# A 31-tap convolution on TensorE: two tiles with four taps stacked on the rows, in place of one tile with diagonals

## The chip, the cores and the metric

The kernel runs on one core of a Trainium2 chip. The metric is the device time of one execution in microseconds; of a kernel the median of several runs is given. The core has five engines that work side by side, each through its own queue in order: TensorE (PE: matmuls; PEld is its weight loads), VectorE (DVE), ScalarE (ACT), GpSimd (POOL) and SyncE (SP), which here issues all transfers between DRAM and the on-chip memory. Matmul results land in PSUM, which has eight banks of 128 rows by 512 float32 values; everything else on chip lies in SBUF, 128 rows wide.

## The reference

One inference step of a two-layer decoder for a prompt of 512 tokens and eight sample sequences of eight tokens, 576 columns in all. Layer 0 mixes with a Conformer convolution and sliding-window attention, layer 1 with a Mamba-2 scan; each layer ends in a gated feed-forward block. What matters here is the Conformer branch of layer 0, cut to its core:

```python
a_val, a_gate, q, k, v = jnp.split(h @ w_in, [...], axis=-1)
u = a_val * jax.nn.sigmoid(a_gate)
padded = jnp.concatenate([conv_hist, u], axis=1)          # 30 earlier rows, then u
c = jax.nn.silu(layernorm(causal_dwconv(padded, conv_w, conv_b), ln_g, ln_b))
...
out = jnp.concatenate([c, o], axis=-1) @ w_out            # o: the attention's output
```

The convolution is depthwise: each of 512 channels has its own 31 taps, and its output at a position is the sum of 31 products over that position and the 30 before it. For the prompt the 30 earlier rows are zeros, for each sample sequence they come from a state.

## The kernel before

Activations lie transposed: channels on the 128 rows, the 576 token columns along the free dimension (512 of the prompt, then 8 x 8 of the samples). The 512 channels of the convolution are four tiles, numbered 0 to 3. Most large matmuls split both float32 factors into a high and a low part and add three products (`mm3`, lines 158 to 160); a plain float32 matmul appears in the trace as two records. Weights come in through `wr` (three buffers), are split by ScalarE (line 148) and VectorE (149) and then used.

`mix0` is the first mixer. `units` projects gate, value, query, key and value tiles from the normalized input. For convolution tile i, `a_gate(i)` makes the sigmoid and `a_val(i)` writes the product u into `cap[i]` (30 columns of zeros, then 512 prompt columns, 542 in all) and into `cas_v[i]` (eight sequences of 30 + 8 columns, 304 in all). Tiles 0 and 2 come first, then q, k and v, then tiles 1 and 3; the value projections of these two run inside the loop over the attention.

Then there are two ways to convolve.

Tiles 0, 2 and 3 run on VectorE. `segment(i)` lets ScalarE copy the tile into 72 overlapping windows of 38 columns (lines 397 and 398), so that prompt and samples have one form, and a later loop makes 31 multiply-adds of 128 x 576 for each tile (lines 681 and 683).

Tile 1 (`PC = 1`) runs on TensorE in `pe_conv`. `cap[1]` is split into a high and a low part, `cph`. For each of the 31 taps ScalarE makes two 128 x 128 diagonals of the tap's weights, high and low (line 522), and TensorE adds three matmuls of 512 columns into one PSUM bank (524 to 526). For the samples ScalarE makes a third diagonal in plain float32 (528), used in a matmul of 64 columns into a second bank (529). VectorE later brings both into `ca[1]` with the bias (673 and 674).

The loop over `todo` goes through eight attention units (four query blocks of 128, two key heads). `scores` multiplies queries and keys (581) into the ring "sc" of three PSUM banks and starts the softmax on VectorE and ScalarE (555 to 566); `values` transposes the probabilities (598), copies them out (600) and multiplies them with the values (602). Values of a unit are written after the scores of the next one. The taps of tile 1 are spread over the last six units. After the loop come the keys and values of the samples' caches (629, 630, loads by SP), their scores (640, 642) and value products (653, 655). At the end the LayerNorm over the four `ca` tiles starts with means by TensorE (691), and `out_proj` multiplies first the attention's output `oh`, then the convolution's output `cc`.

The order in which this is written is not the order in the queues. Before anything runs, a planner goes through the instructions by priority, which is the order of writing, and by the times at which it expects inputs to be ready, and fixes for each engine, SP included, one order. On the chip each engine follows its order and waits at the head of its queue. Buffers named by `self.S` are slots taken from a list in turn, `NSLOT` of them in this phase; a tile written into a slot waits until the slot's earlier readers are done.

Of the kernel before, what the change touches and what calls it, by code (L numbers as in the profile page):

```python
# [25 lines left out]
for _name, _w in (  # L26
    ("norm_e", 8), ("norm_o", 8), ("norm_f0", 8), ("norm_f1", 8),
    ("ca_w", 4 * 31), ("ca_b", 4), ("ln_g", 4), ("ln_b", 4), ("q_g", 1), ("k_g", 1),
    ("fw0", NF * 3), ("fb0", NF), ("fw1", NF * 3), ("fb1", NF),
    ("cc_w", 24 * 4), ("cc_b", 24), ("dsk", 16), ("gn", 16),  # L30
    ("sink_p", 8), ("sink_s", 2), ("dtb", 32), ("alog", 32),
):
    PV[_name] = _n
    _n += _w
# [4 lines left out]
for _name, _w in (  # L39
    ("ident", 128), ("prot", 128), ("blk2", 2), ("amask", 256), ("smask", 2 * 192),  # L40
    ("tri", 128), ("tris", 64), ("bmat", 64), ("bsel", 8), ("selx", 256), ("selm", 128),
    ("sel3", 192), ("bsel3", 4),
):
    CV[_name] = _n
    _n += _w
# [3 lines left out]
class Builder:  # L49
    NSLOT = 50  # L50
    EXTRA = 8
# [298 lines left out]
    def mix0(self):  # L350
# [49 lines left out]
        def a_val(i):  # L400
            def go(half, p):
# [3 lines left out]
                else:  # L405
# [104 lines left out]
        pconv = {}  # L510

        def pe_conv(k0, k1):

            i = PC
            if not pconv:
                pconv[0] = self.pm(), self.pm()
            pp, ps = pconv[0]
            for k in range(k0, k1):
                dg = []
                for w in (cwh, cwl):  # L520
                    dg.append(self.segp.tile([P, P], F32R, tag="dg", bufs=4, name="dg"))
                    nc.scalar.activation(dg[-1], self.ident, AF.Copy, scale=w.bitcast(F32)[:, k:k + 1])
                sl = slice(k, k + NP)
                nc.tensor.matmul(pp, dg[0], cph[0][:, sl], start=k == 0, stop=False)  # L524
                nc.tensor.matmul(pp, dg[0], cph[1][:, sl], start=False, stop=False)
                nc.tensor.matmul(pp, dg[1], cph[0][:, sl], start=False, stop=k == 30)
                df = self.segp.tile([P, P], F32, tag="df", bufs=2, name="df")
                nc.scalar.activation(df, self.ident, AF.Copy, scale=self.pv("ca_w", i * 31 + k))
                nc.tensor.matmul(bt(ps[:, 0:64]), df, cas_v[i][:, :, k:k + 8], start=k == 0, stop=k == 30)
# [94 lines left out]
        values(n, kv, pr)  # L624

# [44 lines left out]
        for i in range(4):  # L670
            if i == PC:
                pp, ps = pconv[0]
                nc.vector.tensor_scalar(ca[i][:, :NP], pp, self.pv("ca_b", i), None, op0=ADD)
                nc.vector.tensor_scalar(ca[i][:, NP:], ps[:, 0:64], self.pv("ca_b", i), None, op0=ADD)
                continue
# [26 lines left out]
        self.free(oh, list(ca.values()), list(cap.values()), cas, lrs, csq, *cph)  # L702
# [406 lines left out]
def build(nc, tc, d):  # L1109
    from contextlib import ExitStack  # L1110
    with ExitStack() as stack:
        b = Builder(nc, tc, d, stack)
        b.setup()
        with tc.tile_pool(name="segp", bufs=1) as b.segp:
            b.phase(b.segp, "prot", "tri")
# [11 lines left out]
def constants():  # L1127
# [12 lines left out]
    put("prot", prot)  # L1140
    half = np.arange(P) // 64
# [125 lines left out]
```

## Time and profile before

| | |
|---|---|
| median of 3 runs | 1622.1 us (1620.45 to 1622.54) |
| the profiled execution | 1617.26 us |
| its span, first to last instruction | 1615.5 us |
| TensorE busy | 1588.7 us (98%) |
| VectorE busy | 1026.3 us (64%) |
| ScalarE busy | 696.5 us (43%) |
| GpSimd busy | 109.4 us (7%) |
| granted TensorE clock, mean | 0.996 |

The profile is of one execution. L158 means line 158 of the kernel before. In a row of groups, `out<-in` names what an instruction writes and reads, xN is the number of instructions, and behind the bar stand busy microseconds in total, the mean of one in nanoseconds, and how long the engine stood idle just before them, with what ended the idling. In a timeline row stand start, duration, engine, line and operation; a bracket at the end gives idle time before it. Matmuls overlap in a pipeline, so the distance between two starts tells more than a duration. Rows of busy time in a stage give the stage, its length, and for PE, PEld, DVE, ACT and POOL the busy time and number of instructions, then the granted clock, the busy share of the DMA engines and GB/s. A row of SPq is SP issuing a transfer; rows of transfers give their number, size, and the median time from issue to landing.

### The profile page before, as it was taken

To read this page: it belongs to the slowest core of one execution; us is meant where nothing else is said; L and a number is where in the kernel's file an instruction comes from. 1 tells how busy PE (TensorE), PEld (TensorE's weight loads), DVE (VectorE), ACT (ScalarE), POOL (GpSimd) and SP (SyncE) were. 2 spreads that over 40 slices of the span, in tenths; PEclk is the share of its full clock that TensorE was granted. 3 is DMA by queue.
4 is the path that set the end of the run, shared out by engine and by line. 5 is a ranking of instruction groups with operands and counts; after the bars stand their busy time and mean duration, and the time that the engine had idled before them with its cause. 6 is when DMAs were issued, how large, how long until landed. Compare 5 with 4: busy or idle time off the path is not lost.

```text
span 1615.5 us, 28735 instructions
## 1 busy us (share of the span) xinstructions
PE 1588.7 (98%) x11704; PEld 1504.8 (93%) x11704; DVE 1026.3 (64%) x1847; ACT 696.5 (43%) x1333; POOL 109.4 (7%) x322
## 2 busy tenths in 40 slices
PE   8999999999999999999999999999899999999999
PEld 8996699999999999998997998998799999999999
DVE  7898677654365355578796676676776653554552
ACT  7248654322122122378766556557352221221220
POOL 0000001000000000010301101101110000000000
PEclk9999999999999999999999999999899999999999
DMA  7222022222222222224335325234222222222222
GB/s 229 71 73 69 1 66 90 80 91 79 80 90 70 93 87 76 83 72 141 132 82 166 102 70 176 92 97 156 97 69 89 91 80 79 92 71 87 92 80 76
DMA packets 63633, 150.05 MB, mean 93 GB/s; under 512 B 18558, under 2 KB 19582, under 8 KB 63502
## 3 DMA queue, kind: packets, MB, share of 16 engines
q1 hardware_dynamic: 63502, 148.23, 28.8%
q8 instruction: 92, 1.51, 0.4%
q14 instruction: 39, 0.32, 0.1%
HBM read 133.86 MB, written 14.34 MB: 92 GB/s over the span
## 4 chain that ended last, share of the span: by engine, by line
PE 89%; DVE 5%; ACT 4%; DMA 2%; issue 1%; POOL 0%; SPq 0%; DVEq 0%; ACTq 0%
PE mm L158 25%; PE mm L160 25%; PE mm L159 25%; DVE cconv L734 1%; DMA acb<-acd 1%; PE yp L974 1%; ACT wh L148 1%; PE pst L923 1%; PE po L602 1%; PE sc L581 1%; PE pt L180 1%; PE pyo L987 1%; PE yp L972 1%; PE mm L524 1%; PE pr L191 1%
## 5 line engine op out<-in xcount | busy, mean ns | idle before, releaser
L158 PE MATMUL mm<-hh,wh 128*128 128x288 f32 (+1 forms) x2288 | 680.6, 298 | 8.4 <-ACT wh L148 7.7
L160 PE MATMUL mm<-hh,wl 128*128 128x288 f32 x2288 | 679.8, 297 | 0.1
L159 PE MATMUL mm<-hl,wh 128*128 128x288 f32 (+1 forms) x2288 | 677.9, 297 | 0.0
L148 ACT ACTIVATE wh<-wr 128x1024 fp32r<-128x1024 f32 (+1 forms) x215 | 223.4, 1039 | 544.1 <-issue 283.3
L158 PEld LDWEIGHTS mm<-hh,wh 128*128 128x128 f32 (+1 forms) x2288 | 429.6, 188 | 14.8 <-ACT wh L148 8.0
L160 PEld LDWEIGHTS mm<-hh,wl 128*128 128x128 f32 x2288 | 429.7, 188 | 4.6 <-issue 2.8
L159 PEld LDWEIGHTS mm<-hl,wh 128*128 128x128 f32 (+1 forms) x2288 | 429.8, 188 | 3.5 <-issue 1.4
L149 DVE TENSOR_TENSOR wl<-wr,wh 128x1024 fp32r<-128x1024 f32 (+1 forms) x215 | 257.7, 1199 | 78.3 <-ACT wh L148 78.1
L158 PE MATMUL mm<-yh,wh 128*128 128x288 f32 x960 | 286.8, 300 | 2.5 <-ACT yh L168 2.5
L159 PE MATMUL mm<-yl,wh 128*128 128x288 f32 x960 | 287.6, 300 | 0.0
L160 PE MATMUL mm<-yh,wl 128*128 128x288 f32 x960 | 286.1, 299 | 0.0
L158 PEld LDWEIGHTS mm<-yh,wh 128*128 128x128 f32 x960 | 182.1, 190 | 6.9 <-issue 3.3
L159 PEld LDWEIGHTS mm<-yl,wh 128*128 128x128 f32 x960 | 182.1, 190 | 4.4 <-issue 3.2
L160 PEld LDWEIGHTS mm<-yh,wl 128*128 128x128 f32 x960 | 181.8, 190 | 2.9 <-issue 2.8
L257 DVE TENSOR_TENSOR x<-x,mm 128x288 f32<-128x288 f32 x192 | 85.7, 451 | 154.8 <-PE mm L160 154.4
L302 DVE TENSOR_TENSOR gbuf<-mm,rs 128x224 f32<-128x224 f32 x44 | 17.2, 392 | 108.0 <-PE mm L160 108.0
L313 ACT ACTIVATE gsilu<-gconv,par 128x512 f32<-128x512 f32 x44 | 31.8, 724 | 115.1 <-DVE gconv L310 115.1
L310 DVE SCALAR_TENSOR_TENSOR gconv<-gbuf,par,gconv 128x592 f32<-128x592 f32 x88 | 73.1, 831 | 1.5
L323 DVE TENSOR_TENSOR gsilu<-mm,gsilu 128x288 f32<-128x288 f32 x88 | 40.0, 455 | 50.3 <-PE mm L160 50.3
L683 DVE SCALAR_TENSOR_TENSOR ca<-seg,par,ca 128x576 f32<-128x576 f32 x90 | 71.3, 810 | 0.3
L734 DVE SCALAR_TENSOR_TENSOR cconv<-cbuf,par,cconv 128x600 f32<-128x600 f32 x72 | 61.4, 856 | 11.6 <-ACT cconv L732 10.6
L955 ACT ACTIVATE ew<-acb,ac 128x128 f32<-128x128 f32 x128 | 41.2, 390 | 37.4 <-DMA acb<-acd 17.6
(315 smaller groups left out, 1735.0 us busy)
## 6 DMA issues: line engine op xcount, KB each, us to landing
wr<-in_w_gate SPq DMA_DIRECT2D x44, 512.0 KB, 3.3
wr<-in_w_up SPq DMA_DIRECT2D x44, 512.0 KB, 3.3
wr<-in_w_in_o SPq DMA_DIRECT2D x40, 512.0 KB, 3.4
wr<-in_w_down SPq DMA_DIRECT2D x32, 448.0 KB, 3.3
wr<-in_w_down SPq DMA_DIRECT2D x16, 512.0 KB, 3.5
acb<-acd SPq DMA_DIRECT2D x32, 256.0 KB, 3.5
h<-in_h SPq DMA_DIRECT2D x32, 256.0 KB, 2.9
out_ssm_s<-h SPq DMA_DIRECT2D x32, 256.0 KB, 2.4
```

Source lines behind the costliest of these rows:

```text
L148: nc.scalar.activation(hi[:, :n], raw[:, :n], AF.Copy)
L149: nc.vector.tensor_tensor(lo[:, :n], raw[:, :n], hi[:, :n].bitcast(F32), op=SUB)
L158: nc.tensor.matmul(out, hi[:, ws], xh[:, sl], start=i == 0, stop=False)
L159: nc.tensor.matmul(out, hi[:, ws], xl[:, sl], start=False, stop=False)
L160: nc.tensor.matmul(out, lo[:, ws], xh[:, sl], start=False, stop=i == n - 1)
L257: nc.vector.tensor_tensor(self.x[m][:, sl], self.x[m][:, sl], p[:, :HB], op=ADD)
L310: nc.vector.scalar_tensor_tensor(cv[:, :592], g[:, k:592 + k], w(k), cv[:, :592], op0=MUL, op1=ADD)
L313: nc.scalar.activation(sl[:, :NP], cv[:, :NP], AF.Silu, bias=b)
L323: nc.vector.tensor_tensor(sl[:, HALF[half]], p[:, :HB], sl[:, HALF[half]], op=MUL)
L683: nc.vector.scalar_tensor_tensor(a, sv[:, :, k:k + 8], w, a, op0=MUL, op1=ADD)
L734: nc.vector.scalar_tensor_tensor(cv[:, :600], g[:, k:600 + k], w(k), cv[:, :600], op0=MUL, op1=ADD)
L955: nc.scalar.activation(ew[:, cs], acb[:, cs], AF.Relu, bias=ac[:, o:o + 1], scale=-1.0)
```

## The change

Two tiles, 1 and 3, are convolved on TensorE (`PC = (1, 3)`), and 0 and 2 on VectorE. The way of tile 1 is replaced. `cap[i]` and `cas_v[i]` of both tiles are stored to DRAM (`cad`). For each column quarter c (32 channels), four copies are loaded back on the 128 rows, copy j shifted by j positions: the prompt's into `xp4[c]`, the samples' into `xs4[c]`, 32 transfers for a tile. So a row block j holds the same 32 channels j positions later, and one matmul with 128 rows adds four taps of 32 channels. Its weights, four 32 x 32 diagonals on top of each other, come from one product on GpSimd for each tile (`w4`) out of a small mask and repacked tap weights (`ca_wq`). Eight such steps make 32 taps (the last has 96 rows, 28 to 30); in each step four matmuls, one for each quarter, write 32 rows of the same PSUM bank. All of it is plain float32; high and low parts, and the diagonals on ScalarE, are gone. The loads of both tiles are written after the value projection of tile 3; then two pieces of the convolution are written in each further attention unit: a piece is two prompt steps, or at the end of a tile all eight sample steps and the two evictions.

The parameter block grows by 128 columns and the constants by 32. In this phase there are 48 slots instead of 50, later 58 in both kernels.

```diff
-        PC = 1
-        cph = self.S("cph", 542, F32R), self.S("cpl", 542, F32R)
-        cwh, cwl = (self.segp.tile([P, 31], F32R, name=n_) for n_ in ("cwh", "cwl"))
-        self.split(self.pv("ca_w", PC * 31, 31), (cwh, cwl), slice(0, 31))
+        PC = (1, 3)
+
+        cad = {i: self.dp.tile([P, 846], F32, name=f"cad{i}") for i in PC}
...
-                    if i == PC:
-                        self.split(cap[i], cph, slice(0, 542))
+                    if i in PC:
+                        nc.sync.dma_start(cad[i][:, 0:542], cap[i])
+                        nc.sync.dma_start(cad[i][:, 542:846].rearrange("p (b c) -> p b c", c=38), cas_v[i])
                     else:
                         segment(i)
...
-        pconv = {}
-
-        def pe_conv(k0, k1):
-
-            i = PC
-            if not pconv:
-                pconv[0] = self.pm(), self.pm()
-            pp, ps = pconv[0]
-            for k in range(k0, k1):
-                dg = []
-                for w in (cwh, cwl):
-                    dg.append(self.segp.tile([P, P], F32R, tag="dg", bufs=4, name="dg"))
-                    nc.scalar.activation(dg[-1], self.ident, AF.Copy, scale=w.bitcast(F32)[:, k:k + 1])
-                sl = slice(k, k + NP)
-                nc.tensor.matmul(pp, dg[0], cph[0][:, sl], start=k == 0, stop=False)
-                nc.tensor.matmul(pp, dg[0], cph[1][:, sl], start=False, stop=False)
-                nc.tensor.matmul(pp, dg[1], cph[0][:, sl], start=False, stop=k == 30)
-                df = self.segp.tile([P, P], F32, tag="df", bufs=2, name="df")
-                nc.scalar.activation(df, self.ident, AF.Copy, scale=self.pv("ca_w", i * 31 + k))
-                nc.tensor.matmul(bt(ps[:, 0:64]), df, cas_v[i][:, :, k:k + 8], start=k == 0, stop=k == 30)
+
+        w4 = {}
+        for i in PC:
+            w4[i] = self.segp.tile([P, 1024], F32, name=f"w4{i}")
+            nc.gpsimd.tensor_tensor(w4[i].rearrange("p (k m) -> p k m", m=32),
+                                    self.cv("m32", 0, 32).unsqueeze(1).broadcast_to([P, 32, 32]),
+                                    self.pv("ca_wq", i * 32, 32).unsqueeze(2).broadcast_to([P, 32, 32]), op=MUL)
+
+        def pe_conv(i):
+            xp4 = [self.S("xp4", 540) for _ in range(4)]
+            xsp = [self.S("xs4", 576) for _ in range(2)]
+            xs4 = [xsp[c // 2][:, (c % 2) * 288:(c % 2) * 288 + 288].rearrange("p (b t) -> p b t", t=36) for c in range(4)]
+            src = cad[i]
+            for c in range(4):
+                for j in range(4):
+                    n = 540 if j < 3 else 536
+                    m = 36 if j < 3 else 32
+                    r, rc = slice(j * 32, j * 32 + 32), slice(c * 32, c * 32 + 32)
+                    nc.sync.dma_start(xp4[c][r, 0:n], src[rc, j:j + n])
+                    nc.sync.dma_start(xs4[c][r, :, 0:m],
+                                      src[rc, 542:846].rearrange("p (b t) -> p b t", t=38)[:, :, j:j + m])
+            yield
+            pp, ps = self.pm(), self.pm()
+            for s in range(8):
+                k = slice(0, P if s < 7 else 96)
+                for c in range(4):
+                    w = w4[i][k, (s * 4 + c) * 32:(s * 4 + c) * 32 + 32]
+                    nc.tensor.matmul(pp[c * 32:c * 32 + 32, :], w, xp4[c][k, 4 * s:4 * s + NP], start=s == 0, stop=s == 7)
+                if s % 2:
+                    yield
+            for s in range(8):
+                k = slice(0, P if s < 7 else 96)
+                for c in range(4):
+                    w = w4[i][k, (s * 4 + c) * 32:(s * 4 + c) * 32 + 32]
+                    nc.tensor.matmul(bt(ps[c * 32:c * 32 + 32, 0:64]), w, xs4[c][k, :, 4 * s:4 * s + 8],
+                                     start=s == 0, stop=s == 7)
+            nc.vector.tensor_scalar(ca[i][:, :NP], pp, self.pv("ca_b", i), None, op0=ADD)
+            nc.vector.tensor_scalar(ca[i][:, NP:], ps[:, 0:64], self.pv("ca_b", i), None, op0=ADD)
+            self.free(xp4, xsp)
+            yield
...
+        convs = iter(())
         for t_, it in enumerate(todo):
             ready.append((it, scores(*it)))
             if t_ in (0, 1):
                 self.units([val_unit((1, 3)[t_])], 1)
                 if t_:
                     self.norm_end()
+                    convs = [pe_conv(i) for i in PC]
+                    for c_ in convs:
+                        next(c_)
+                    convs = itertools.chain(*convs)
             else:
-                pe_conv((t_ - 2) * 31 // 6, (t_ - 1) * 31 // 6)
+                next(convs, None)
+                next(convs, None)
```

More of the change, by code (lines that the diff above doesn't have):

```diff
@@ L39 @@
 for _name, _w in (
-    ("ident", 128), ("prot", 128), ("blk2", 2), ("amask", 256), ("smask", 2 * 192),
+    ("ident", 128), ("m32", 32), ("prot", 128), ("blk2", 2), ("amask", 256), ("smask", 2 * 192),
     ("tri", 128), ("tris", 64), ("bmat", 64), ("bsel", 8), ("selx", 256), ("selm", 128),
@@ L624, in mix0 @@
         values(n, kv, pr)
+        for _ in convs:
+            pass
         kct = [self.S("kct", 512) for _ in range(2)]
@@ L701, in mix0 @@
         self.out_proj([d["w_out_e"][1, c] for c in range(4)], oh, 4)
-        self.free(oh, list(ca.values()), list(cap.values()), cas, lrs, csq, *cph)
+        self.free(oh, list(ca.values()), list(cap.values()), cas, lrs, csq)
         self.norm_begin("norm_f0", True)
@@ L1140, in constants @@
     put("prot", prot)
+    put("m32", np.tile(np.eye(32, dtype=f), (4, 1)))
     half = np.arange(P) // 64
```

18 lines of the change are left out of this document (10 added, 8 removed).

## The prediction

> **What bounds the kernel now.** I read the totals of the page first, then its chain of waits, then busy times by stage around the convolution.
>
> ```profile
> span 1615.5 us, 28735 instructions
> PE 1588.7 (98%) x11704; PEld 1504.8 (93%) x11704; DVE 1026.3 (64%) x1847; ACT 696.5 (43%) x1333; POOL 109.4 (7%) x322
> ...
> PE 89%; DVE 5%; ACT 4%; DMA 2%; issue 1%; POOL 0%; SPq 0%; DVEq 0%; ACTq 0%
> ```
>
> TensorE is busy for 98% of the span and holds 89% of the chain. So a change counts as far as it shortens TensorE's queue or fills its few gaps. The convolution's last value projection ends near 116.5 us, and the attention's output projection gets going near 197.5 us; between the two lie the attention, the TensorE convolution of tile 1 and the start of the LayerNorm. Stages of the busy times:
>
> ```profile
> core 0: us, PE busy (x) PEld busy (x) DVE busy (x) ACT busy (x) POOL busy (x), PEclk, DMA share, GB/s
> ...
> 116.50:172.00 55.50, 55.50 (x283) 36.67 (x282) 45.41 (x155) 44.25 (x140) 0.00 (x0) 1.00 0.21 62
> 172.00:197.50 25.50, 22.60 (x122) 14.81 (x120) 14.05 (x40) 18.25 (x67) 0.00 (x0) 0.93 0.00 1
> ```
>
> Up to 172 us TensorE has no gap at all, although VectorE (45.4 of 55.5 us) and ScalarE (44.3) are also heavily used. After 172 us it stands for 2.9 us, and its granted clock falls to 0.93. TensorE's timeline shows what one tap of the present convolution takes, and where the gap is:
>
> ```profile
> 121.14 0.47 PE L524 MATMUL mm<-cph,dg 128*128 128x512 f32 x1
> ...
> 121.93 0.34 PE L529 MATMUL mm<-cas,df 128*128 128x64 f32 x2
> 122.07 0.48 PE L524 MATMUL mm<-cph,dg 128*128 128x512 f32 x1
> ...
> 174.59 0.80 PE L524 MATMUL mm<-cph,dg 128*128 128x512 f32 x1 [2.19 <-ACT dg L522]
> ...
> 176.31 0.77 PE L524 MATMUL mm<-cph,dg 128*128 128x512 f32 x1
> ...
> 177.98 0.47 PE L524 MATMUL mm<-cph,dg 128*128 128x512 f32 x1
> ...
> 197.83 0.40 PE L159 MATMUL mm<-ol,wh 128*128 128x288 f32 x1 [0.69 <-DVE ol L169]
> ```
>
> From one tap's first matmul to the next is 122.07 - 121.14 = 0.93 us. At 172.4 us TensorE waits 2.19 us for a diagonal that ScalarE has not made yet, and the two taps after it take 177.98 - 174.59 = 3.39 us instead of 1.86, the price of a clock that fell in the gap.
>
> **What goes.** All 31 taps of tile 1 as diagonals: 31 x 0.93 = 28.8 us of TensorE's queue. With them go the diagonals on ScalarE, so the wait of 2.19 us and the slow 1.5 us behind it lose their cause. Out of TensorE's path: 28.8 + 2.2 + 1.5 = 32.5 us. From the groups of this stage, the other engines' share:
>
> ```profile
> L683 DVE SCALAR_TENSOR_TENSOR ca<-seg,par,ca 128x576 f32<-128x576 f32 x43 | 34.6, 813 | 0.2
> ...
> L522 ACT ACTIVATE dg<-ident,cwh 128x128 fp32r<-128x128 f32 x29 | 11.6, 401 | 4.3 <-PE mm L525 4.2
> L528 ACT ACTIVATE df<-ident,par 128x128 f32<-128x128 f32 x29 | 11.4, 394 | 0.0
> ...
> L397 ACT ACTIVATE seg<-cap 128x2432 f32<-128x2432 f32 x1 | 2.2, 2221 | 0.0
> ...
> L673 DVE TENSOR_SCALAR ca<-mm,par 128x512 f32<-128x512 f32 x1 | 0.8, 750 | 2.0 <-PE mm L526 2.0
> ```
>
> VectorE loses tile 3's 30 multiply-adds, 30 x 0.81 = 24.4 us, and gains one more eviction of 0.75 us with its small partner. ScalarE loses 93 diagonals of about 0.39 to 0.40 us, some 37 us, and the 2.2 us copy into overlapping windows. I count none of this directly, since TensorE has no gap before 172 us. It matters as slack: about 36 of VectorE's 59 us and 25 of ScalarE's 62 us stay in the stage.
>
> **What is added on TensorE.** Per tile 8 steps; in each, four matmuls of 128 rows by 32 columns over 512 positions, one for each column quarter, and the same for the 64 sample positions. The nearest rows are the readout of the state in the second mixer, which has exactly this form, and the value matmuls and sample scores of the attention:
>
> ```profile
> 763.86 1.07 PE L987 MATMUL pyo<-h,cfm 128*32 128x512 f32 x8
> 764.85 0.74 PE L994 MATMUL pst<-x,b 96*128 96x512 f32 x2
> ...
> 118.58 1.07 PE L602 MATMUL po<-ptb,vt 128*64 128x512 f32 x2
> ...
> 128.14 1.07 PE L602 MATMUL po<-ptb,vt 128*64 128x512 f32 x2
> ...
> 151.84 0.40 PE L640 MATMUL sc<-kct,qss 64*32 64x128 f32 x2
> ...
> 181.76 1.93 PE L602 MATMUL po<-ptb,vt 128*64 128x512 f32 x4
> 183.63 1.09 PE L598 MATMUL pt<-ident,sm 128*128 128x128 f32 x8
> ...
> 162.03 0.42 PE L640 MATMUL sc<-kct,qss 64*32 64x128 f32 x8
> 162.38 0.43 PE L642 MATMUL sc<-kf,qss 64*128 64x64 f32 x2
> ...
> 189.11 0.65 PE L655 MATMUL po<-ptb,vc 128*64 128x32 f32 x8
> 189.70 0.43 PE L653 MATMUL po<-ptb,vts 64*64 64x128 f32 x2
> ```
>
> A float32 matmul shows as two records. Two value matmuls over 512 positions that follow each other take 183.63 - 181.76 = 1.87 us, 0.93 each. Four on the column quarters take 764.85 - 763.86 = 0.99 together: the quarters do run side by side. Hence 16 groups x 0.99 = 15.8 us (16 x 0.93 = 14.9 from below, if the switch into quarters is what the 0.06 us more are). No row has four quarters over 64 positions. Four over 128 take 0.35 us; four that follow each other over 32 take 0.59. I take 0.35, the form with quarters: 16 x 0.35 = 5.6 us. From above it is 16 x 0.59 = 9.4 us; from below half the positions, 16 x 0.18 = 2.9. Together 21.4 us, between 17.8 and 25.2.
>
> The Trainium skill (TensorE: Matmul & The Clock Gate, Measured speedup vs the span model) speaks against full concurrency: three column tiles of 32 over 512 positions gained 2.38, not 3. Carried over to four as an estimate (3.17), a group would take 1.17 us and the sum would be 2.9 us worse; the row gives 3.76 of 4, and the measurement decides.
>
> **The loads.** The quarters need each channel group four times, shifted by one position, on 128 rows. So each tile goes to DRAM and comes back in 32 transfers (16 prompt, 16 sample), all issued by SP. Rows of SP's queue and of the transfers:
>
> ```profile
> 2.12 1.85 SPq L121 DMA_DIRECT2D x<-in_x  x4
> ...
> 12.78 0.56 SPq L377 DMA_DIRECT2D cas<-in_ca_hist  x1
> 13.45 1.75 SPq L139 DMA_DIRECT2D wr<-in_w_in_e  x2
> ...
> 109.94 0.54 SPq L409 DMA_DIRECT2D out_ca_s<-cas  x1
> ...
> 118.30 0.54 SPq L409 DMA_DIRECT2D out_ca_s<-cas  x1
> ...
> 124.88 0.33 SPq L629 DMA_DIRECT2D kct<-in_kct  x1
> ...
> acb<-acd SPq DMA_DIRECT2D x32, 256.0 KB, 3.5
> ...
> kct<-in_kct SPq DMA_DIRECT2D x2, 256.0 KB, 2.7
> ...
> out_ca_s<-cas SPq DMA_DIRECT2D x4, 120.0 KB, 5.2
> ```
>
> Plain loads are issued 1.85 / 4 = 0.46 us apart, one in short pieces holds SP for 13.45 - 12.78 = 0.67. A pair costs 1.13 us of SP, a tile 16 x 1.13 = 18 us. (The DMA engines keep up: 1024 short pieces land 2.5 us later than a plain load of twice the size, 5.2 against 2.7; the 256 of one such load would take a quarter of that, 0.6.) Tile 1 is complete at 109.9; its store follows at 110.5 and, like the sample store of the same size in short pieces, lands after 5.2 us, near 116. Issued from then to 134, its loads have landed 3.5 us later (as the loads that come back from DRAM in the second mixer), near 138. Tile 3's are issued to 152 and there near 156. Behind them in SP's order stand the cached keys and values, now issued at 124.9; at 152 they would land near 155, against sample scores that start at 151.8 now. That is some 3 us late for a chain whose last value matmuls above come after 189 us.
>
> What hides the loads is attention. TensorE's 78.1 us in the stage hold 28.8 + 1.5 of convolution, so 47.8 us of other work, more than the 39.5 us from 116.5 to 156, and tile 1's 10.7 us are free from 138. If TensorE never stood, the stage would be 47.8 + 21.4 = 69.2 us instead of 81, an end at 186. But the order in TensorE's queue is fixed before the run. A convolution step that stands in it ahead of its data holds up every score, transpose and value matmul behind it, and through them the softmax on VectorE and ScalarE. No row shows 32 such loads in a burst. From below the wait is 0 (the cover above). From above the first step stands where the first tap stands now, 120.2 us, and waits until 138: 18 us. I take one wait of the size of the old one with its slow clock, 3.7 us: nearer to 0, because the cover is larger than the need and each TensorE wait for a transfer in this profile is under a microsecond.
>
> ```profile
> PEld pyo L987 <- DMA h<-in_h: 1.6, 2, 0.8
> ...
> L995 POOL TENSOR_TENSOR h<-h,cds 128x512 f32<-128x512 f32 x32 | 37.6, 1195 | 180.4 <-PE pyo L987 139.5 <-DMA wr<-in_w_in_o 33.2 <-DMA h<-in_h 6.6
> ```
>
> GpSimd's two products of 1024 columns take about 2 x 1.2 = 2.4 us each by the row of half their width; GpSimd is idle throughout the stage and they need only parameters, so they cost nothing here, and 5 us at most if they came last. The second tile's convolution waits for the first one's eviction from the same two PSUM banks, about 1 us, with attention to do meanwhile.
>
> **The sum.** 21.4 + 3.7 - 32.5 = -7.4 us. The profiled execution took 1617.3 us (span 1615.5 and 1.8 around it), which is 4.8 us under the median of the runs; I apply the difference to the median: 1622.1 - 7.4 = 1614.7.
>
> **The rivals.**
> 1. More than the sum: TensorE never stands and the stage ends at 186; ScalarE, freed of its diagonals, also takes away the 0.69 us at the end. That is 81 - 69.2 = 11.8, or 15.4 with the lower bounds of the groups (17.8 instead of 21.4): about 1608. For it: two of three loaded engines get lighter by 40% or more. Against: the loads.
> 2. The wait eats the gain: the loads come 8 to 13 us after the place of the first step, or the attention's own chain (score, softmax, transpose, value) becomes the bound when TensorE has less to put between. 11.1 - 11 = 0: 1622. For it: attention units now follow each other 128.14 - 118.58 = 9.6 us apart, and no row shows them closer over a longer stretch.
> 3. Slower: the convolution steps stand in TensorE's queue where the taps stand now, and TensorE waits there for the burst of 32 issues on SP. Price 18 + 1.5 for the clock, less 11.1: +8.4, so 1630.5. It decides from a wait of 11 us. For it: 18 us of issue for each tile is certain in order of size. Against: 47.8 us of attention is available.
> 4. The quarters don't overlap when they accumulate over eight steps: 64 x 0.93 = 59.5 instead of 15.8, +44 - 7: 1658. Only the missing accumulation in the nearest row speaks for it.
>
> **How the numbers follow.** Forecast 0.40 (1611 to 1618.5, from the bounds of the sample groups and a wait of 0 to 7 us), rival 1 0.23, rival 2 0.20, rival 3 0.14, rival 4 0.03. A difference below 0.2%, 3.2 us, I take as not told from none. Faster are the forecast and rival 1, less a little of the forecast's edge: 0.62. Same: rival 2 and that edge, 0.20. Slower: rivals 3 and 4 and the upper edge of rival 2, 0.18. The range for 8 in 10 goes from 1607 to 1626: it leaves out rival 4, most of rival 3 and little below rival 1.
>
> **What would show it.** Right: groups of eight records on quarters over 512 positions 0.9 to 1.0 us apart, no diagonals on ScalarE, 30 fewer multiply-adds on VectorE after 116 us, output projection of the attention starting near 190. SP: two bursts of about 18 us. Wrong: a TensorE wait for the shifted tiles of over 11 us, with the granted clock down behind it; quarter groups near 3.7 us; or a TensorE that stands for scores and softmax while the loads have long landed.

## The result, and the profile after

The change makes the kernel slower. Its median is 1630.75 us (1626.99 to 1636.6, 5 runs) against 1622.1 us before, a ratio of 1.0056 with an interval of 1.0034 to 1.0079. The forecast was 1614.7 us. The profiled execution took 1628.89 us.

The totals of the page after:

```profile
span 1626.7 us, 28923 instructions
PE 1586.7 (98%) x11805; PEld 1493.1 (92%) x11805; DVE 1007.6 (62%) x1816; ACT 668.7 (41%) x1238; POOL 115.5 (7%) x324
```

TensorE is busy 2 us less than before and the span is 11.2 us longer, so it stands 13.2 us longer; and its mean granted clock in this execution is 0.991, before 0.996. By the marks of the table further down, 5.2 of the 11.2 us lie ahead of the first attention score, none between it and the attention's output projection (95.3 us in both kernels, where the forecast expected a gain), 1.9 from there to the mark of layer 0, and 4.1 behind that mark. There the code is the same and executions of these kernels differ by up to 8 us, so the 4.1 stay unexplained. Two places can be explained.

**The first: 16 to 22 us, before any convolution.** The timeline after, at the start of the first projections (start, duration, engine, line, operation):

```profile
15.99 5.54 POOL L516 TENSOR_TENSOR w<-cst,par 128x1024 f32<-128x1024 f32 x2 [14.73 <-DMA cst<-in_cst]
...
16.61 0.75 DVE L206 TENSOR_TENSOR ssq<-ssq,sq 128x576 f32<-128x576 f32 x1
...
17.29 2.47 DVE L360 SCALAR_TENSOR_TENSOR hl<-x,par,hh 128x576 fp32r<-128x576 f32 x1
...
19.68 2.46 DVE L206 TENSOR_TENSOR ssq<-ssq,sq 128x576 f32<-128x576 f32 x1
19.81 0.40 PE L161 MATMUL mm<-hl,wh 128*128 128x288 f32 x1 [1.33 <-DVE hl L360]
...
22.29 1.15 PE L182 MATMUL pt<-o,ssq 128*96 128x1 f32 x12 [1.54 <-DVE ssq L206]
```

and the same instructions before:

```profile
17.30 0.81 DVE L358 SCALAR_TENSOR_TENSOR hl<-x,par,hh 128x576 fp32r<-128x576 f32 x1
...
18.03 0.75 DVE L204 TENSOR_TENSOR ssq<-ssq,sq 128x576 f32<-128x576 f32 x1
...
18.99 1.10 PE L180 MATMUL pt<-o,ssq 128*96 128x1 f32 x12
```

The two GpSimd products that make the weights (`w4`) run here, because they need only parameters. Beside them two VectorE instructions take 2.47 and 2.46 us instead of 0.81 and 0.75. TensorE waits for both, and the sums of squares start at 22.29 instead of 18.99 us. The Trainium skill (SBUF — State Buffer, SBUF: two separate sides) describes this: a VectorE instruction with two SBUF inputs and a GpSimd instruction share a port pair that whoever starts first holds for its whole length. The rows agree in the main: both VectorE operations have two inputs, and they take 2.47 - 0.81 = 1.66 and 2.46 - 0.75 = 1.71 us longer, while the two products take 5.54 us together. Not every such operation is held up: the one at 16.61 us took its usual 0.75, although the record of the first product begins at 15.99.

**The second: the end of the attention.** Busy times by stage after (stage, length, then PE, PEld, DVE, ACT, POOL, granted clock, DMA share, GB/s):

```profile
160.00:180.00 20.00, 18.29 (x178) 6.75 (x170) 3.60 (x15) 5.50 (x17) 0.00 (x0) 1.00 0.53 167
180.00:200.00 20.00, 20.00 (x201) 14.44 (x191) 6.75 (x38) 7.15 (x27) 0.00 (x0) 0.79 0.00 1
200.00:220.00 20.00, 19.14 (x117) 17.83 (x118) 12.25 (x27) 11.63 (x26) 0.96 (x6) 0.79 0.09 27
```

and the same stages before:

```profile
160.00:180.00 20.00, 17.80 (x91) 12.29 (x90) 15.91 (x41) 14.09 (x48) 0.00 (x0) 0.91 0.00 0
180.00:200.00 20.00, 18.96 (x119) 12.24 (x118) 11.07 (x29) 13.40 (x45) 0.00 (x0) 1.00 0.01 2
200.00:220.00 20.00, 19.99 (x157) 19.58 (x157) 14.85 (x35) 11.60 (x26) 0.59 (x6) 1.00 0.07 24
```

From 160 to 200 us VectorE is busy for 10.4 and ScalarE for 12.7 us, before for 27.0 and 27.5. The granted clock is 0.79 from 180 to 220, before 1.00. As an estimate, a busy TensorE gets 40 x 0.21 = 8.4 us less done there than at full clock. That is more than its added waits: between the first score and the output projection TensorE stands 5.9 us, before 2.6. What lowers the clock, no run here isolates. The timeline shows what VectorE and ScalarE wait for:

```profile
133.37 1.82 PE L539 MATMUL mm<-xp,w 128*32 128x512 f32 x2 [2.65 <-DMA xp<-cad]
...
158.12 6.63 PE L539 MATMUL mm<-xp,w 128*32 128x512 f32 x57
164.16 0.31 PE L546 MATMUL mm<-xs,w 128*32 128x64 f32 x6
164.37 0.42 DVE L577 CUSTOM_DVE_ANT_0 sm<-sc,cst 128x256 f32<-128x256 f32 x1 [6.38 <-PE mm L539]
164.41 1.09 ACT L622 ACTIVATE ptb<-pt 128x512 f32<-128x512 f32 x2 [6.42 <-PE mm L539]
...
165.02 1.06 PE L546 MATMUL mm<-xs,w 128*32 128x64 f32 x52
...
166.07 1.02 PE L539 MATMUL mm<-xp,w 128*32 128x512 f32 x2
...
182.21 0.75 DVE L548 TENSOR_SCALAR ca<-mm,par 128x512 f32<-128x512 f32 x1 [11.28 <-PE mm L539]
182.90 0.42 PE L670 MATMUL sc<-kct,qss 64*32 64x128 f32 x8
...
201.51 1.09 PE L160 MATMUL mm<-oh,wh 128*128 128x288 f32 x2
```

The matmuls are cheap: 57 records in 164.16 - 158.12 = 6.04 us, 0.85 for eight, and 52 sample records in 166.07 - 165.02 = 1.05 us, 0.16 for eight. TensorE's wait for the copies is 2.65 us. But at 164.4 us the softmax (`sm`) and the copy of the probabilities (`ptb`) have stood 6.4 us for a convolution that they have no data from: their slots held tile 1's shifted copies. And the scores of the samples, which before started at 151.8 us among the attention's other work, start at 182.90 with no prompt attention left beside them. SP's queue, timeline and then its waits, shows why:

```profile
122.35 0.33 SPq L530 DMA_DIRECT2D xp<-cad  x1
...
158.19 0.42 SPq L531 DMA_DIRECT2D xs<-cad  x1
158.65 0.45 SPq L530 DMA_DIRECT2D xp<-cad  x1
159.14 0.42 SPq L531 DMA_DIRECT2D xs<-cad  x1
166.11 0.35 SPq L659 DMA_DIRECT2D kct<-in_kct  x1
```

```profile
SPq L659 <- PE mm L546: 6.5, 1, 6.5
```

The 64 loads keep SP until 159.6 us; the cached keys come behind them and then wait 6.5 us more, again for a slot, until the convolution's sample matmuls have read it.

### The profile page after: what moved, and what is told of

The parts are those of the page before. It is cut to its first block, busy times and chain, and to the rows that moved or that the text cites. A ratio compares the mean times of both kernels' runs of the same rounds, so it can differ in the third digit from the quotient of the medians.

```text
span 1626.7 us, 28923 instructions
## 1 busy us (share of the span) xinstructions
PE 1586.7 (98%) x11805; PEld 1493.1 (92%) x11805; DVE 1007.6 (62%) x1816; ACT 668.7 (41%) x1238; POOL 115.5 (7%) x324
## 4 chain that ended last, share of the span: by engine, by line
PE 84%; DVE 3%; DMA 3%; ACT 3%; issue 1%; SPq 0%; POOL 0%; DVEq 0%; ACTq 0%; POOLq 0%
PE mm L160 25%; PE mm L161 25%; PE mm L162 25%; DMA acb<-acd 2%; PE mm L539 1%; PE yp L1001 1%; PE pt L182 1%; PE pst L950 1%; PE yp L999 1%; ACT wh L150 1%; PE po L624 1%; PE pt L937 1%; PE pr L193 1%; DMA h<-in_h 1%; PE pyo L1014 1%
## 5 line engine op out<-in xcount | busy, mean ns | idle before, releaser
L259 DVE TENSOR_TENSOR x<-x,mm 128x288 f32<-128x288 f32 x192 | 85.6, 452 | 156.0 <-PE mm L162 155.8
L1022 POOL TENSOR_TENSOR h<-h,cds 128x512 f32<-128x512 f32 x32 | 36.9, 1173 | 184.1 <-PE pyo L1014 179.0
```

The costliest lines, as they stand in the source:

```text
L259: nc.vector.tensor_tensor(self.x[m][:, sl], self.x[m][:, sl], p[:, :HB], op=ADD)
L1022: nc.gpsimd.tensor_tensor(hp(h0[b4]), hp(h0[b4]), cds[:, b * 32 + 8 * g:b * 32 + 8 * g + 8].unsqueeze(2).broadcast_to([P, 8, 64]), op=MUL)
```

## The experiments

All times are compared by ratio with the kernel before on the same chip. It had medians of 1619.69 to 1622.19 us beside the experiments, so medians of runs on different chips are compared by their ratios. The marks are from each profiled execution, in us: first attention score, first score of the samples, start of the attention's output projection, and the store of the feed-forward block's state near the end of layer 0 ("layer 0").

| kernel | median | ratio to before (95%) | score | samples | out proj. | layer 0 |
|---|---|---|---|---|---|---|
| before | 1622.1 | | 101.0 | 151.8 | 196.3 | 613.1 |
| after | 1630.75 | 1.0056 (1.0034 to 1.0079) | 106.2 | 182.9 | 201.5 | 620.2 |
| a1_w4_late | 1624.57 | 1.0023 (1.0007 to 1.0039) | 102.5 | 185.1 | 200.8 | 618.1 |
| a2_products_alone | 1625.37 | 1.0031 (1.0018 to 1.0044) | 104.5 | 155.3 | 199.9 | 616.7 |
| b48_slots_alone | 1620.62 | 0.9991 (0.9974 to 1.0007) | 102.5 | 153.4 | 198.0 | 614.5 |
| a4_no_round_trip | 1612.5 | 0.9937 (0.9914 to 0.9961) | 102.6 | 164.4 | 189.4 | 605.9 |
| a5_held_slots | 1617.43 | 0.9989 (0.9975 to 1.0003) | 102.8 | 175.2 | 189.7 | 612.1 |
| a3_caches_early | 1619.59 | 1.0001 (0.9989 to 1.0013) | 102.3 | 159.5 | 194.9 | 609.7 |
| a9_merged_loads | 1622.27 | 1.0008 (0.9994 to 1.0022) | 102.1 | 176.4 | 192.1 | 610.3 |
| a8_fewer_loads | 1614.18 | 0.9959 (0.9946 to 0.9973) | 102.4 | 145.7 | 191.4 | 608.2 |
| a8_again | 1613.25 | 0.9953 (0.9935 to 0.9970) | 102.7 | 145.2 | 187.7 | 606.1 |
| b3_prompt_from_sbuf | 1612.77 | 0.9954 (0.9937 to 0.9971) | 102.0 | 156.0 | 185.6 | 605.3 |
| a10_one_tile | 1615.61 | 0.9971 (0.9955 to 0.9987) | 102.3 | 170.5 | 188.1 | 609.6 |
| b1_one_tile_all | 1605.91 | 0.9917 (0.9895 to 0.9938) | 101.4 | 144.1 | 178.1 | 606.5 |
| b1_again | 1607.8 | 0.9929 (0.9904 to 0.9954) | 101.5 | 142.4 | 177.9 | 606.9 |
| b6_one_tile_early | 1611.88 | 0.9942 (0.9921 to 0.9964) | 101.4 | 152.3 | 177.2 | 605.1 |
| c1_no_vector_taps | 1597.65 | 0.9856 (0.9831 to 0.9882) | 101.4 | 142.4 | 174.0 | 592.5 |
| c2_no_tensor_taps | 1610.4 | 0.9940 (0.9918 to 0.9962) | 102.0 | 144.5 | 183.5 | 601.7 |

From the mark of layer 0 to the end of the span the code is the same; it takes 1001.6 to 1009.6 us in these executions. So single marks and medians can differ by some microseconds.

### GpSimd's products

a1_w4_late: the weights in slots of the list, in four products of 512 columns, so that they can't run before slots come free.

```diff
-            w4[i] = self.segp.tile([P, 1024], F32, name=f"w4{i}")
-            nc.gpsimd.tensor_tensor(w4[i].rearrange("p (k m) -> p k m", m=32), ...)
+            w4[i] = [self.S("w4", NP) for _ in range(2)]
+            for h in (0, 1):
+                nc.gpsimd.tensor_tensor(w4[i][h].rearrange("p (k m) -> p k m", m=32), ...)
```

> The changed kernel, with the tap weights' products on GpSimd put into slots that come free only in the middle of the projections (near 80 us), as four products of 512 columns. Theory A (GpSimd's product at 16 to 21.5 us slows VectorE while the first normalization is on the path): the first attention score, at 106.2 us in the changed kernel, comes back to about 101, and the time falls by 4 to 6 us, to 1625 to 1627. Theory B (the loss lies in the loads and waits of the convolution stage alone): no change, 1629 to 1632.

a2_products_alone: the kernel before, with four products of that size written at the same place, whose results nothing reads.

```diff
+        w4 = self.segp.tile([P, 512], F32, name="w4")
+        for i in range(4):
+            nc.gpsimd.tensor_tensor(w4.rearrange("p (k m) -> p k m", m=32), ...)
```

> The kernel before, with four GpSimd products of 512 columns added (as many elements as the two of the change) whose result nobody reads; nothing else is changed. Theory A: they run as soon as the constants are there, near 16 to 20 us, VectorE's multiply-adds beside them take about 2.4 us instead of 0.8, and the time rises by 3 to 6 us, to 1625 to 1628. Theory B: GpSimd is idle there and nothing waits for it: 1622, within 2.

Moving the products brings the ratio from 1.0056 to 1.0023 (5.4 us at 1622 us); the two intervals overlap a little, and the first score comes 3.7 us earlier. Adding the products to the kernel before costs 0.0031 (5.0 us), clear of noise, and moves the first score by 3.5 us. The timeline of a2_products_alone shows the same coupling, with products of half the size:

```profile
15.92 5.75 POOL L534 TENSOR_TENSOR w<-cst,par 128x512 f32<-128x512 f32 x4 [14.66 <-DMA cst<-in_cst]
...
16.11 1.61 DVE L358 SCALAR_TENSOR_TENSOR hl<-x,par,hh 128x576 fp32r<-128x576 f32 x1
17.65 1.60 DVE L204 TENSOR_TENSOR ssq<-ssq,sq 128x576 f32<-128x576 f32 x1
```

The VectorE instructions take 1.61 - 0.81 = 0.80 and 1.60 - 0.75 = 0.85 us longer, half of the 1.66 and 1.71 beside products twice as wide: what is added follows the product. (The expectation had 2.4 us, the length beside the wide ones.) In a1_w4_late the products run between 80.8 and 95.5 us.

b48_slots_alone: the kernel before with 48 slots and 10 later, as the change has them.

```diff
-    NSLOT = 50
-    EXTRA = 8
+    NSLOT = 48
+    EXTRA = 10
```

> The kernel before with 48 slots in the first mixer and 10 later ones instead of 50 and 8, and nothing else. In the changed kernel the second mixer is 3.5 us longer, and ScalarE waits there 38 us for loads of decays instead of 18. If the order in which slots are handed on does that: 1624 to 1627. If it comes from elsewhere (the order in which the changed first mixer gives its slots back, or chance): 1622, within 2.

The interval contains 1. The smaller list alone costs nothing that can be told.

### The way through DRAM as a whole

a4_no_round_trip: a1_w4_late without the stores and the 64 loads; the matmuls, as many and as large, read the unshifted values, so the convolutions of tiles 1 and 3 are not computed.

```diff
-                nc.sync.dma_start(xp4[c][r, 0:n], src[rc, j:j + n])
-                nc.sync.dma_start(xs4[c][r, :, 0:m], ...)
+            xp4, xs4 = [cap[i]] * 4, [cas_v[i]] * 4
```

> As a1, but the trip through DRAM is left out: no stores, none of the 64 loads; the matmuls on column quarters read the tile and its sample part where they lie, so what tiles 1 and 3 get is not the convolution, at the same number and size of matmuls. If the loads and the order that follows from them cost the gain of the convolution stage: 1611 to 1618, that is 8 to 14 us under a1. If the stage is bound by the attention's own chain: within 3 us of a1, 1623 to 1627.

0.0086 (13.9 us) below a1_w4_late by the ratios, 12.1 us by the medians on one chip (1624.57 - 1612.5). Without the round trip the change gains 10.2 us (0.0063) on the kernel before; loads, slots and the order behind them cost more than that. The next three runs take this apart.

### Slots, caches, number of loads

a5_held_slots: the copies' and weights' slots are given back only after the samples' attention, from a list of 51.

```diff
-            self.free(xp4, xsp, w4[i])
+            held_c.append((xp4, xsp, w4[i]))
```

> The kernel of a1_w4_late with the slots of the shifted copies and of the weights held until after the samples' attention (51 slots for this phase in place of 48), so that no softmax tile of a later unit takes a slot that tile 1's or tile 3's matmuls still read. In a1_w4_late ScalarE stood 10.10 us for TensorE's convolution matmuls ahead of such a tile, and the stage from the first attention score to the FFN's output took 515.6 us. Theory A (the slots couple softmax to the convolution): that wait goes, the stage falls by 5 to 10 us, the time to 1615 to 1620. Theory B (the caches of the samples are loaded behind 64 loads in SyncE's queue): the samples' scores still start near 185 us, the time stays within 2 us of 1624.6. Theory C (the loads land late for TensorE, which stands for them with the rest of its queue behind): the wait of TensorE for a load stays, time within 2 us of 1624.6.

a3_caches_early: loads and stores of the caches ahead of the 64 loads.

```diff
                     self.norm_end()
+                    kct = [self.S("kct", 512) for _ in range(2)]
+                    vc = [self.S("vc", 512) for _ in range(2)]
+                    for i in range(2):
+                        nc.sync.dma_start(kct[i], d["kct"][i])
...
                     convs = [pe_conv(i) for i in PC]
```

> The kernel of a1_w4_late with the four loads of the samples' caches and the four stores behind them written ahead of the convolution's 64 loads, on the same queue. In a1_w4_late they are issued from 154.1 us on, in the kernel without the round trip from 134.5. Theory A (slots): time within 2 us of 1624.6, since the softmax still waits. Theory B (caches late): they are issued near 119 us, the samples' scores start 15 us or more before 185, time 1613 to 1618; the convolution's loads come some 4 us later. Theory C (loads late): the loads come later still, by about 8 issues of 0.46 us or 4 us, and the time rises by 2 to 4 us to 1627 to 1629.

a9_merged_loads: 24 loads for a tile, whole shifted rows of the samples for two quarters in one.

```diff
-                    nc.sync.dma_start(xs4[c][r, :, 0:m], ...)
+                    if c % 2:
+                        nc.sync.dma_start(xsp[c // 2][r, :].rearrange("p (c n) -> p c n", n=304)[:, :, 0:304 - j], ...)
```

> The kernel of a1_w4_late with one edit: 24 in place of 32 loads for each tile (the samples' copies as whole shifted rows, two quarters in one load, none of 128 or 144 bytes). Slots are coupled and caches late as there. Theory C (the number of loads itself, because they land late): SyncE issues 16 loads fewer or some 7.5 us less, tile 3's copies land and the caches are issued 7 us earlier, time 1617 to 1621, ratio 0.998 to 1.000. Theory A and B together, with the number of loads of no weight of its own: only the caches profit, 1 to 3 us, time 1621 to 1624, ratio about 1.001.

Waits of a1_w4_late (in total, times, longest), which go in a5_held_slots:

```profile
ACT ptb L623 <- PE mm L540: 10.1, 1, 10.1
...
DVE sm L578 <- PE mm L540: 6.6, 1, 6.6
```

Holding the slots, with three more in the list, gives 0.0034 back (5.5 us), and the attention's output projection starts 11.1 us earlier; the caches are still issued at 154.2 us. Early caches give 0.0022 (3.6 us), only just clear of noise: the samples' scores start 25.6 us earlier, while VectorE's part of the softmax stands longer for the convolution than in a1_w4_late, by the waits of a3_caches_early:

```profile
DVE sm L578 <- PE mm L540: 20.0, 2, 11.3
```

Merged loads give 0.0015 (2.4 us), which the intervals don't tell from none; in that run the caches are issued at 146.7 instead of 154.1 us, and the mark of layer 0 comes 7.8 us earlier in the profiled execution. So slots and caches are both causes and neither is the whole; what the number of loads weighs is not settled. The wait of TensorE for the copies, which theory C of the expectations was built on, is 2.0 us in a1_w4_late.

a8_fewer_loads: all three edits.

> The kernel of a1_w4_late with both former edits (slots held, caches first) and with 24 in place of 32 loads for each tile: the samples' shifted copies are loaded as whole shifted rows, two quarters in one load, with no pieces of 128 or 144 bytes. SyncE issues 48 loads in about 22 us in place of 31. Theory A or B alone: time as in the run that undoes that cause, 1613 to 1620. Theory C (loads late): tile 3's loads are complete some 9 us earlier less the 4 us of the caches, time 2 to 5 us below a3_caches_early and a5_held_slots. If all three add up: near the 1612.5 us of the kernel without the round trip, plus about 2.

0.0064 below a1_w4_late (10.4 us), about the sum of the three (11.5), and not to be told from a4_no_round_trip. It beats the kernel before by 0.0041 or 6.7 us, where the forecast had 7.4.

The granted clock goes the same way. Each run has a mean clock on record; its median is 0.996 to 0.997 for the kernel before on the chip of each experiment, 0.989 for the changed kernel, 0.991 for a1_w4_late, 0.992 for a9_merged_loads, 0.995 for a5_held_slots, 0.996 for a3_caches_early and 0.997 for a8_fewer_loads. As an estimate for a TensorE that is nearly always busy, 0.006 of 1624 us is 9.7 us, close to the 10.4 that the three edits give back. So most of what the waits cost appears to reach the time as a lower clock. That the waits lower it is not shown.

b3_prompt_from_sbuf takes the store ahead of the prompt's loads away too:

```diff
-                    nc.sync.dma_start(xp4[c][r, 0:n], src[rc, j:j + n])
+                    nc.sync.dma_start(xp4[c][r, 0:n], cap[i][rc, j:j + n])
```

> The kernel of a8_fewer_loads with the prompt's shifted copies loaded straight from the values in SBUF (32 loads again in place of 32 from DRAM, and the two stores of 542 columns gone); only the samples' copies still go through DRAM. If the store ahead of the loads is what TensorE's waits for the copies (2.8 us in a8_fewer_loads) come from: 1 to 3 us below a8_fewer_loads, 1611 to 1613. If not: level with it within 1.5 us.

Level with it, 0.9954: the prompt's detour through DRAM costs nothing that can be told.

### One tile or two

a10_one_tile is a1_w4_late, and b1_one_tile_all is a8_fewer_loads, with tile 3 back on VectorE. b6_one_tile_early is the latter with tile 1's loads written right after its values.

```diff
-        PC = (1, 3)
+        PC = (1,)
```

> The kernel of a1_w4_late with tile 1 alone by quarters and tile 3 back on VectorE, as it is in the kernel before: 32 loads in place of 64. VectorE has 31 taps of 0.93 us or 28.8 us more than in a1_w4_late in the stage, and TensorE one tile of about 8 us in place of two. Theory A and B: half of the slots, and the caches 15 us earlier: the round trip's 12 us fall to 4 or less, but VectorE's taps are on the path again: about the kernel before, 1618 to 1622. If VectorE's taps are not what sets the end of this stage at all, and the burst is: faster than before, 1612 to 1617. Theory C with a wait for the first loads alone: 1622 to 1626.

> The kernel of a8_fewer_loads with tile 1 alone by quarters, tile 3 on VectorE. If VectorE's 31 taps of tile 3 lie on the path once slots and caches are free: 5 to 10 us above a8_fewer_loads, 1618 to 1624. If TensorE sets the end and VectorE's taps lie beside it: level with a8_fewer_loads or up to 5 us below (one convolution of about 8 us and 24 loads fewer), 1609 to 1614.

> The kernel of b1_one_tile_all with tile 1's loads written right after tile 1's values, ahead of tile 3's value unit and of the caches, so that they are issued some 8 us earlier. If TensorE's wait for the copies costs (theory C): 1 to 3 us below b1_one_tile_all. If not: level with it within 1.5 us.

a10_one_tile falls below both the kernel before and a1_w4_late (0.9971), though SP stands 29.8 us for a slot ahead of the caches there, as its waits show:

```profile
SPq L660 <- PE mm L540: 29.8, 1, 29.8
```

With slots and caches mended too, b1_one_tile_all is the fastest, 0.9917. Its expectations had a gain of at most 5 us on a8_fewer_loads; by the ratios it is 6.8 us. Loads that are issued earlier bring nothing that can be told (0.9942, intervals overlap). In a8_fewer_loads tile 3's matmuls come last of all:

```profile
181.65 7.60 PE L540 MATMUL mm<-xp,w 128*32 128x512 f32 x57
...
190.53 1.24 PE L720 MATMUL pm<-ca,o 128*128 128x288 f32 x4
191.39 0.51 PE L160 MATMUL mm<-oh,wh 128*128 128x288 f32 x1
```

That is 190.53 - 181.65 = 8.9 us of TensorE. But the marks of layer 0 of the two kernels differ by 1.7 us only, and b1_one_tile_all shows why:

```profile
178.10 0.80 PE L160 MATMUL mm<-oh,wh 128*128 128x288 f32 x4 [1.23 <-ACT oh L170]
...
202.59 0.81 DVE L712 SCALAR_TENSOR_TENSOR ca<-seg,par,ca 128x576 f32<-128x576 f32 x1
204.50 3.00 DVE L722 TENSOR_TENSOR ca<-ca,pm 128x288 f32<-128x288 f32 x8
...
218.00 0.85 PE L160 MATMUL mm<-ch,wh 128*128 128x288 f32 x2 [0.52 <-ACT ch L170]
```

The output projection begins 13.3 us earlier, but VectorE's last tap ends at 203.4 us, and the projection of the convolution's half, behind the LayerNorm, starts at 218.0. Two runs take the shares apart: c1_no_vector_taps leaves out 30 of tile 3's taps on VectorE, c2_no_tensor_taps seven eighths of its matmuls on TensorE, each beside its full kernel on one chip.

```diff
-            for k in range(31):
+            for k in range(1 if i == 3 else 31):
```

```diff
-            for s in range(8):
+            for s in range(8 if i == 1 else 1):
```

> The kernel of b1_one_tile_all unchanged, beside a8_again on the same chip and for the two runs that leave work out. b1_one_tile_all stood at 0.9917 of the kernel before and a8_fewer_loads at 0.9959, but in their profiled executions the stage from the first score to the FFN's output differs by 0.7 us only (505.1 and 505.8). If tile 3's place decides: 5 to 9 us below a8_again. If the difference was chance: within 2 us of it.

> The kernel of a8_fewer_loads unchanged. Tile 3's place decides: 0.995 to 0.997 of the kernel before, 5 to 9 us above b1_again. Chance: within 2 us of b1_again.

> The kernel of b1_one_tile_all with 30 of tile 3's 31 taps left out on VectorE (its convolution is then not computed beyond one tap). In b1_one_tile_all VectorE's last tap ends at 203.4 us, some 25 us after the attention's output projection has begun, and TensorE then stands for the LayerNorm in several pieces, with a granted clock of 0.50 in the 10 us from 210 on. If the 24 us of taps are hidden beside the output projection: within 1.5 us of b1_again. If they are late and set the LayerNorm: 3 to 8 us below it.

> The kernel of a8_fewer_loads with tile 3's matmuls cut to one step in eight (its convolution is then not computed beyond four taps); all loads, slots and waits for them stay. In a8_fewer_loads these matmuls run from 181.65 to 190.5 us with nothing of the attention left beside them. If TensorE's 8.9 us lie on the path: 6 to 8 us below a8_again. If VectorE or the LayerNorm sets the end there: within 2 us of it.

VectorE's taps are not free. Without them the time falls by 10.2 us by the medians (1607.8 to 1597.65; 0.0073 by the ratios) and the mark of layer 0 by 14.4, more than was expected for late taps. The attention's output projection starts 3.9 us earlier, and the convolution's at 206.21 us instead of 218.21:

```profile
206.21 0.30 PE L160 MATMUL mm<-ch,wh 128*128 128x288 f32 x1
```

Without TensorE's matmuls it falls by 2.9 us (1613.25 to 1610.4), which the intervals don't tell from none and which lies between the two expectations; layer 0's mark falls by 4.4 (606.1 to 601.7), less than the 7.8 us that are left out. b1 lies 0.0042 (6.8 us, on two chips) below a8 in one comparison and 0.0024 (3.9 us; 5.5 by the medians) in the other, which alone is not clear of noise. In the profiled executions some 4 us of the lead lie behind layer 0, where their code is the same: 1002.2 and 1001.6 us against 1006.3 and 1005.2. Why that part differs stays open, and so does how much of the lead is due to the tile's place.

## Why the prediction was wrong

The step that failed is the price of the round trip. The sum charges the stores, the 64 loads, their slots and the order behind them with one TensorE wait of 3.7 us; by a4_no_round_trip against a1_w4_late they cost 0.0086, 13.9 us. A second step failed beside it: GpSimd's products, put at nothing, cost 5.4 us. In the order of the prediction:

- **What goes on TensorE, 32.5 us.** The diagonals and their waits are gone. a4_no_round_trip, without loads, came 10.2 us (0.0063) below the kernel before, against 32.5 - 21.4 = 11.1 in the sum. That this is so near is luck: with the 16.2 us that the next point has for 21.4, it should have been 16.3, which lies outside a4's interval (6.3 to 13.9 us). Some 6 us of the gain did not arrive. In a4's profiled execution the granted clock is 0.68 from 180 to 200 us, by estimate 20 x 0.32 = 6.4 us; what lowered it is open.

```profile
180.00:200.00 20.00, 20.00 (x118) 18.15 (x118) 8.40 (x19) 8.51 (x20) 0.99 (x6) 0.68 0.00 1
```

- **What is added on TensorE, 21.4 us.** Too much. Groups take 0.85 us and not 0.99, sample groups 0.16 and not 0.35: 16 x 0.85 + 16 x 0.16 = 16.2 us, below the lower bound of 17.8. The estimate of 1.17 us from the Trainium skill (TensorE: Matmul & The Clock Gate, Measured speedup vs the span model) was further off than the row. This error was in the change's favour. Rival 4 is out: the quarters do overlap while they accumulate.
- **SP's issue.** A pair was put at 1.13 us and takes 159.14 - 158.19 = 0.95 in the bursts; with the stores and a late start the 64 loads run to 159.6 us, forecast 152. Of this, 5.2 us come from the first place.
- **One wait of 3.7 us.** TensorE's own wait for the copies was sized well (2.65 us) and is a small part of the loss. What the round trip does cost was put aside a few lines above it: caches that come "some 3 us late for a chain whose last value matmuls above come after 189 us". They came 41 us later in SP's order (166.1 for 124.9), the samples' scores 31 us, and it is those scores that fill TensorE between the prompt's units; a3_caches_early got 3.6 us back. That they would also wait for a slot was not thought of.
- **The slots.** No term had them. The page before could not show this wait, but the rule was in front of the reader: a tile written into a slot waits for the slot's earlier readers, and `self.free(xp4, xsp)` gives six slots of each tile to the softmax of the units that follow, whose writes then stand behind matmuls that stand behind loads. 5.5 us by a5_held_slots.
- **GpSimd's products "cost nothing here".** They were weighed against the stage of the convolution, where GpSimd is idle. But what needs only parameters runs at the start, and there the question was not GpSimd's time but VectorE's. 5.4 us by a1_w4_late, 5.0 by a2_products_alone; the bound "5 us at most" came near the size by luck, for another place and cause, and the sum took zero.
- **VectorE's 24 us, counted at nothing.** In c1_no_vector_taps 30 such taps are worth 10.2 us once TensorE has been relieved. Slack in a stage's total says nothing on whether the last tap is late for the LayerNorm. Here the sum left out a gain, as far as this carries over to the changed kernel, which no run shows.

Put together by the ratios: 1614.7, and 0.9 for the gain without the round trip (10.2 for 11.1), 10.2 for the round trip (13.9 for 3.7) and 5.4 for the products, is 1631.2, which is 1622.1 x 1.0056. It comes out by construction, since the three differences follow each other from kernel to kernel, and each is known to 4 or 5 us either way. Of the 13.9 us, slots, caches and loads give back 11.5 if they are added up, 10.4 together.

Rival 3 named almost the right time (1630.5) by luck, for a reason that the runs refute: TensorE stood 2.65 us for the loads, not the 11 from which that rival decides. Rival 2's half-sentence, that the attention's own chain becomes the bound, is nearer: TensorE waits for softmax that waits for slots, if only for about a microsecond at a time. The forecast's time was met by a8_fewer_loads (0.9959, and 1614.7 / 1622.1 = 0.9954), after the products and three causes of delay that it had not priced were taken away. Since its other terms were off too, that does not confirm them.

## What to carry to other kernels

When a change puts new tiles into a shared list of slots, follow each freed slot to its next writer, and when it puts loads into a queue, follow what stood behind them: here both led to the attention, which had nothing to do with the convolution. Place an instruction that needs only parameters by when it can start, not by where its result is used, and look at which engine it shares a port with there. A tile that moves from one engine to another should be tried on each side with its work left out; here that priced one side (10.2 us) and left the other within noise. And the mean granted clock should be compared beside the waits: short waits of TensorE here went with a loss larger than their length.

## What the runs showed of the hardware

- A GpSimd product of two SBUF operands can hold up a VectorE instruction of two SBUF operands: beside products of 1024 columns 1.66 and 1.71 us were added to instructions of 0.81 and 0.75, beside products of 512 columns 0.80 and 0.85. Two products of 1024 columns cost the whole kernel 5.4 us, four of 512 columns 5.0.
- Four matmuls of 128 rows by 32 columns over 512 positions take 0.85 us together at full clock, 0.16 over 64 positions. In a8_fewer_loads, at a granted clock of 0.91 for the 20 us around them, 57 records took 188.66 - 181.65 = 7.01 us, 0.98 for eight.
- The mean granted clock differs from kernel to kernel: 0.986 to 0.992 in the five runs of the changed kernel, 0.994 to 1.000 in the eighteen of a8_fewer_loads and a8_again, which have the same matmuls. Within one execution it fell to 0.79 for 40 us while TensorE was busy for 39.1 of them. Why is not shown.
